# Gated delta rule on one Trainium2 core: the inverse of a 128-token chunk assembled ahead by two products for pairs of heads

## The chip, the cores and the metric

One core of a Trainium2 chip runs the whole layer in one launch. The metric is device time in microseconds (us), the median of three runs. TensorE is called PE below, VectorE DVE, ScalarE ACT, GpSimd POOL; SP is the queue from which this kernel issues all its DMAs.

## What is computed

The layer has a gated DeltaNet branch and a stick-breaking attention branch; both are projected, gated, merged and projected out. The change lies in the DeltaNet branch. For each of 4 heads a state of 128x128 is carried over chunks of the 2048 tokens; within a chunk a unit lower triangular system is solved:

```python
m = where(strict, beta[..., :, None] * kk * decay, 0.0)
sol = triangular_solve(eye + m, rhs, left_side=True, lower=True, unit_diagonal=True)
...
def step(state, inp):
    v_new = u_c - einsum('bhck,bhkv->bhcv', w_c, state)
    o = einsum('bhck,bhkv->bhcv', qd_c, state) + einsum('bhij,bhjv->bhiv', qk_c, v_new)
    state = state * ge_c[..., None, None] + einsum('bhck,bhcv->bhkv', kd_c, v_new)
    return state, o
```

The kernel works with chunks of 128 tokens, 16 in all (the reference's are 64; the result is the same).

## The kernel before

**Stages.** Projections of all columns of the input come first (tiles `pj`; weights and activations are split in two parts, so three matmuls stand for one product). While the last attention projections run, `dn_solve` (L671 to L711) inverts on DVE the two 64x64 diagonal blocks of all 16 x 4 triangular systems at once, one (chunk, head) in each partition, and stores them transposed in the scratch tensor `d_tt`. Then come attention, the recurrence over chunks (`dn_states`, L713) mixed with the last gate projections (`pj`) and with the up-projections (`up`, L913, tiles `y`), the rest of the up-projections, and the output projection (tiles `o`).

**One chunk** is `dn_chunk` (L780). `mm4` (L772) makes one product for each of the 4 heads, in plain f32, into one PSUM bank; a tile called `dn` is such a bank. A chunk has seven of them:

- two with `kq` and the state: the right-hand side `rn` (DVE, L788) and the first part of the output `o` (L791); POOL then scales the state (L792);
- three to apply the inverse: `tt` (the two 64x64 inverses on the diagonal) times `rn`, copied to `v1` by ACT (L796); `mo` (the coupling block, its only nonzero quarter) times `v1`, added to `rn` by DVE (L799); and `tt` times `rn` again, scaled into `w2` and `w` (L803, L804);
- one with `kt` that updates the state (L807), and one with `qk` that completes `o` (L809). POOL, ACT and DVE then normalise `o` (L811 to L819); four PE transposes and a store follow later (`tail`, L821).

**Loads.** `dn_load` (L752) brings a chunk's `kq`, `vn`, `tt` (two DMAs), `kt`, `qk` and `za`; `kq`, `vn`, `qk` and `za` have one buffer each. `mo` is loaded in `dn_chunk`.

**Order.** Each `yield` of `dn_chunk` ends a step; `dn_states` lets at least `LD` = 1.1 us of PE work of other kinds be recorded between two steps. PE work is chained in the order of recording, so PE's order is fixed: steps of the recurrence with groups of 6 `pj` matmuls or 12 `y` matmuls between them. Each other engine and SP run their instructions in one order too. `up` of 256 tokens may begin once the outputs of its two chunks are stored.

Of the kernel before, what the change touches and what calls it, by code (L numbers as in the profile page):

```python
# [8 lines left out]
F32 = mybir.dt.float32  # L9
# [4 lines left out]
ALU = mybir.AluOpType  # L14
# [4 lines left out]
P = 128  # L19
# [6 lines left out]
NH = 4  # L26
NC = S // P
# [3 lines left out]
HB = 64  # L31
# [6 lines left out]
class Block:  # L38


    def __init__(self, ctx, tc, ins, out):
        self.ctx, self.tc, self.nc = ctx, tc, tc.nc
        self.i = ins
        self.out = out
        dr = ctx.enter_context(tc.tile_pool(name="dr", bufs=1, space=DRAM))

        def scratch(name, n, shape):
            return [dr.tile(shape, F32, name=f"{name}{i}") for i in range(n)]

        self.d_kq = dr.tile([NC, P, NH, 2, P], F32, name="d_kq")  # L50
        self.d_kt = dr.tile([NC, P, NH, P], F32, name="d_kt")
        self.d_vn = dr.tile([NC, P, NH, P], F32, name="d_vn")
        self.d_qk = dr.tile([NC, P, NH, P], F32, name="d_qk")
        self.d_mt = dr.tile([NC, NH, P, P], F32, name="d_mt")
        self.d_tt = dr.tile([NC, NH, 2, HB, HB], F32, name="d_tt")
        self.d_za = scratch("d_za", NC, [P, NH * P])
        self.d_q = dr.tile([2, SH * SD, S], F32, name="d_q")
        self.d_k = dr.tile([2, SH * SD, S], F32, name="d_k")
        self.d_v = dr.tile([SH, P, NT, P], F32, name="d_v")
        self.d_zb = scratch("d_zb", 4, [P, S])  # L60
        self.d_g = scratch("d_g", S // OG, [P, KB, 2, OG])
        self.d_oa = dr.tile([4, P, S], F32, name="d_oa")
        self.d_ob = dr.tile([4, P, S], F32, name="d_ob")
        self.d_m = dr.tile([S // OG, P, KB, OG], F32, name="d_m")
        self.now, self.pending, self.back, self.credit, self.rate = 0, [], None, 0.0, 0.0
        self.op, self.lead, self.slot = None, 0, 0
        self.chain, self.last, self.clock, self.attended, self.zb_done = False, None, 0.0, False, 0
        self.consts()
# [602 lines left out]
    def dn_solve(self):  # L671
# [31 lines left out]
            nc.gpsimd.affine_select(bt, bt, pattern=[[-1, H], [1, n]], compare_op=ALU.not_equal, fill=1.0, base=0, channel_multiplier=0)  # L703
        zero = wk.tile([P, H, H], F32, name="zero", bufs=1)
        nc.vector.memset(zero, 0.0)
        for b in range(2):
            ls = slice(L * b, L * b + L)
            nc.sync.dma_start(t[:, b, 0:H], b1[ls])
            nc.sync.dma_start(t[:, b, H:HB, H:HB], b2[ls])
            nc.sync.dma_start(t[:, b, H:HB, 0:H], zero[ls])  # L710
        yield 1.0  # L711

    def dn_states(self):  # L713
# [1 line left out]
        st = wk.tile([P, NH, P], F32, name="state", bufs=1)  # L715
        nc.vector.memset(st, 0.0)
        tts = [wk.tile([P, NH, P], F32, name=f"tt{k}", bufs=1) for k in range(2)]
        mo = wk.tile([P, NH, P], F32, name="mo", bufs=1)
        for t in tts + [mo]:
            nc.gpsimd.memset(t, 0.0)  # L720
        tails, self.stored = [], 0

# [8 lines left out]
                self.stored += 1  # L731
                yield 0.0

        loads = self.dn_load(0, tts[0])
        yield from self.wait(self.clock + 9.0)
        for c in range(NC):
            yield from store(1)
            cur = loads
            steps = self.dn_chunk(c, cur, st, mo)
            for n, _ in enumerate(steps):  # L740
                if n == 1 and c + 1 < NC:
                    loads = self.dn_load(c + 1, tts[(c + 1) % 2])
                yield from store(2)
                yield 0.0
                yield from self.wait(self.clock + self.LD)
            tails.append((self.clock + 11, self.dn_tail))
        yield from store()

    def dt(self, name, n):
        return self.dk.tile([P, NH, P], F32, tag=name, name=name, bufs=n)  # L750

    def dn_load(self, c, tt):  # L752
        nc = self.nc
        kq = self.dk.tile([P, NH, 2, P], F32, tag="kq", name="kq", bufs=1)
        kt, vn, qk, za = self.dt("kt", 2), self.dt("vn", 1), self.dt("qk", 1), self.dt("za", 1)
        nc.sync.dma_start(kq, self.d_kq[c])
        nc.sync.dma_start(vn, self.d_vn[c])
        for b in range(2):
            bs = slice(HB * b, HB * b + HB)
            nc.sync.dma_start(tt[bs, :, bs], self.d_tt[c, :, b].rearrange("h x i -> x h i"))  # L760
        nc.sync.dma_start(kt, self.d_kt[c])
        nc.sync.dma_start(qk, self.d_qk[c])
        nc.sync.dma_start(za, self.d_za[c].rearrange("p (h d) -> p h d", h=NH))
        return kq, kt, vn, qk, za, tt

    def bank(self):
        return self.pt.tile([P, NH, P], F32, tag="tp", name="dn")
# [9 lines left out]

    LD = 1.1

    def dn_chunk(self, c, loads, st, mo):  # L780

        nc = self.nc
        kq, kt, vn, qk, za, tt = loads
        nc.sync.dma_start(mo[0:HB, :, HB:P], self.d_mt[c, :, 0:HB, HB:P].rearrange("h j i -> j h i"))
        ps = self.mm4(lambda h: kq[:, h, 0], lambda h: st[:, h])
        rn = self.dt("rn", 1)
        for h in range(NH):
# [2 lines left out]
        o = self.dt("o", 2)  # L790
        nc.vector.tensor_tensor(o, ps, self.bc(self.egc, c), ALU.mult)  # L791
        nc.gpsimd.tensor_tensor(st, st, self.bc(self.ge, c), ALU.mult)  # L792
        yield
        ps = self.mm4(lambda h: tt[:, h], lambda h: rn[:, h])
        v1 = self.dt("v1", 1)
        nc.scalar.copy(v1, ps)  # L796
        yield
        ps = self.mm4(lambda h: mo[:, h], lambda h: v1[:, h])
        nc.vector.tensor_tensor(rn, ps, rn, ALU.add)  # L799
        yield  # L800
        ps = self.mm4(lambda h: tt[:, h], lambda h: rn[:, h])
        w, w2 = self.dt("w", 1), self.dt("w2", 1)
# [430 lines left out]
```

## Time and profile before

| | |
|---|---|
| median of 3 runs | 2068.93 us (2068.79 to 2069.32) |
| profiled execution | 2067.06 us, its span 2065.3 us |
| PE busy | 2017.7 us, 98% of the span |
| DVE, POOL, ACT busy | 1399.9, 1023.6, 933.2 us |
| granted TensorE clock, mean | 0.997 of full |
| DMA | 286.71 MB, 139 GB/s over the span |
| recurrence, first to last `dn` instruction | 1535.8 to about 1784 us |

The span runs from the first to the last instruction; 1.8 us lie around it. A busy PE is not a PE at its peak: matmuls overlap, and what a group costs is read from where the next one starts. A row of the trace names the line, the engine, the operation and out<-in; an idle time in brackets or behind a bar is that just before the instruction, with what ended it.

### The profile page before, as it was taken

What the parts mean: (1) busy time and instruction counts of PE and PEld (TensorE: products, weight loads), DVE (VectorE), ACT (ScalarE), POOL (GpSimd) and SP (SyncE); (2) the same over time, 40 slices, a digit from 0 to 9 for tenths busy, and PEclk for the clock granted to TensorE, in tenths of its full rate; (3) what the DMA queues carried; (4) which work ended last, traced back from release to release, by engine and by line L of the source; (5) the groups of instructions that cost most, each with busy time, mean ns of one, the idle gap of its engine ahead of it and who ended that gap; (6) DMA issues with size and microseconds to landing.
All of it is one profiled execution on the core that took longest, in us unless ns stands there. A gap on an engine that the chain in (4) does not pass through costs nothing. (4 is left out here: it accounts for less than half of the span.)

```text
span 2065.3 us, 36611 instructions
## 1 busy us (share of the span) xinstructions
PE 2017.7 (98%) x12831; PEld 1810.2 (88%) x12831; DVE 1399.9 (68%) x2559; ACT 933.2 (45%) x1933; POOL 1023.6 (50%) x1200
## 2 busy tenths in 40 slices
PE   7999999999999999999999999999999999999999
PEld 7987887789999988888888888888888889999887
DVE  7356777777999318888888877877744466443753
ACT  6335655322222117767667766766733321211321
POOL 4336776533443205555555555555537654533564
PEclk9999999999999999999999999999999999999999
DMA  7213333226333553344664443443347787655552
GB/s 244 66 57 106 114 108 97 80 79 128 104 122 113 149 139 106 112 123 114 162 180 133 135 116 104 115 114 104 101 132 225 220 263 230 205 189 163 204 193 102
DMA packets 273511, 286.71 MB, mean 139 GB/s; under 512 B 48752, under 2 KB 206640, under 8 KB 272176
## 3 DMA queue, kind: packets, MB, share of 16 engines
q1 hardware_dynamic: 273328, 284.38, 46.4%
q8 instruction: 102, 1.67, 0.3%
q14 instruction: 81, 0.66, 0.1%
HBM read 181.54 MB, written 102.76 MB: 138 GB/s over the span
## 5 line engine op out<-in xcount | busy, mean ns | idle before, releaser
L1184 POOL TENSOR_TENSOR s<-s,r 128x512 f32<-128x512 f32 (+2 forms) x320 | 306.5, 958 | 321.5 <-DVE r L1180 315.1
L124 PE MATMUL pj<-xh,whi 128*128 128x512 f32 x1024 | 422.5, 413 | 1.9 <-DVE one L1053 1.9
L124 PE MATMUL pj<-xh,wlo 128*128 128x512 f32 x1024 | 405.4, 396 | 0.0
L124 PE MATMUL pj<-xl,whi 128*128 128x512 f32 x1024 | 404.8, 395 | 0.0
L124 PE MATMUL pj<-whi,xh 128*128 128x256 f32 (+1 forms) x1024 | 293.2, 286 | 1.0 <-ACT xh L380 1.0
L1180 DVE TENSOR_TENSOR_SCAN r<-z,carry,zero 128x512 f32<-128x512 f32 x192 | 245.8, 1280 | 69.2 <-ACT z L1178 57.7
L124 PE MATMUL pj<-wlo,xh 128*128 128x256 f32 (+1 forms) x1024 | 289.6, 283 | 0.2 <-DVE wlo L330 0.2
L124 PE MATMUL pj<-whi,xl 128*128 128x256 f32 (+1 forms) x1024 | 289.7, 283 | 0.0
L1177 ACT ACTIVATE s<-z 128x512 f32<-128x512 f32 (+2 forms) x320 | 171.5, 536 | 140.0 <-PE z L124 62.2
L124 PEld LDWEIGHTS pj<-xh,wlo 128*128 128x128 f32 x1024 | 192.9, 188 | 44.1
L124 PEld LDWEIGHTS pj<-xh,whi 128*128 128x128 f32 x1024 | 193.5, 189 | 28.9 <-issue 2.1
L124 PEld LDWEIGHTS pj<-xl,whi 128*128 128x128 f32 x1024 | 194.0, 189 | 27.4
L124 PEld LDWEIGHTS pj<-whi,xh 128*128 128x128 f32 x1024 | 194.2, 190 | 1.4 <-ACT xh L380 1.4
L124 PEld LDWEIGHTS pj<-wlo,xh 128*128 128x128 f32 x1024 | 194.4, 190 | 0.5 <-DVE wlo L330 0.5
L124 PEld LDWEIGHTS pj<-whi,xl 128*128 128x128 f32 x1024 | 194.0, 190 | 0.3 <-DVE xl L381 0.3
L1200 DVE TENSOR_TENSOR lo<-at,hi 128x512 fp32r<-128x512 f32 (+1 forms) x288 | 183.8, 649 | 14.1 <-ACT hi L1199 13.3
L124 PE MATMUL z<-kt,qt 128*128 128x512 f32 (+3 forms) x640 | 187.2, 374 | 0.9 <-DVE r L1180 0.6
L1199 ACT CAST hi<-at 128x512 fp32r<-128x512 f32 (+1 forms) x288 | 159.3, 566 | 60.3 <-PE at L128 55.2
L330 POOL TENSOR_TENSOR wlo<-wraw,whi 128x512 fp32r<-128x512 f32 (+2 forms) x66 | 115.8, 1755 | 123.6 <-ACT whi L329 102.7
L1178 ACT ACTIVATE z<-z 128x512 f32<-128x512 f32 (+2 forms) x320 | 170.4, 532 | 0.0
L128 PE MATMUL at<-ident,s 128*128 128x128 f32 x1088 | 165.2, 274 | 1.2 <-DVE lo L1200 0.5
L124 PE MATMUL y<-xh,xh 128*128 128x256 f32 x512 | 149.6, 292 | 3.2 <-DVE yt L929 3.2
(219 smaller groups left out, 4329.1 us busy)
## 6 DMA issues: line engine op xcount, KB each, us to landing
kt<-d_k SPq DMA_DIRECT2D x160, 128.0 KB, 2.9
vt<-d_v SPq DMA_DIRECT2D x80, 256.0 KB, 3.6
xt<-in_x_dram SPq DMA_DIRECT2D x32, 512.0 KB, 4.3
qt<-d_q SPq DMA_DIRECT2D x64, 256.0 KB, 5.4
d_g<-sg SPq DMA_DIRECT2D x128, 128.0 KB, 2.3
gt<-d_g SPq DMA_DIRECT2D x64, 256.0 KB, 3.3
wraw<-in_w_in_dram SPq DMA_DIRECT2D x56, 256.0 KB, 3.3
wraw<-in_w_in_dram SPq DMA_DIRECT2D x18, 512.0 KB, 4.0
```

The costliest lines, as they stand in the source:

```text
L124: self.pin(self.nc.tensor.matmul(out, lhsT, rhs, **kw))
L128: self.pin(self.nc.tensor.transpose(*args))
L330: (eng or nc.gpsimd).tensor_tensor(lo[:, ks, :n], raw[:, :, :n], hi[:, ks, :n].bitcast(F32), ALU.subtract)
L1177: nc.scalar.activation(s[:, :w], z[:, :w], AF.Sigmoid, scale=SD ** -0.5)
L1178: nc.scalar.activation(z[:, :w], z[:, :w], AF.Sigmoid, scale=-(SD ** -0.5))
L1180: nc.vector.tensor_tensor_scan(r[:, 0:w][:, ::-1], z[:, 0:w][:, ::-1], self.zero.to_broadcast([P, w]), init, ALU.mult, ALU.add)
L1184: nc.gpsimd.tensor_mul(s[:, :w], s[:, :w], r[:, 1:w + 1])
L1199: nc.scalar.copy(hi[:, c:], flat[:, c:])
L1200: nc.vector.tensor_tensor(lo[:, c:], flat[:, c:], hi[:, c:].bitcast(F32), ALU.subtract)
```

## The change

For a chunk the inverse of a 2x2 block triangular matrix is [[T1, 0], [N21, T2]], N21 a product of T2, the coupling block and T1. The change makes that corner ahead. `dn_solve` also writes the first 64x64 inverse of each system untransposed to a new scratch tensor `d_tn`: 32 small copies on ACT and 16 DMAs, through three slots of the scratch tile `stmp`. The new `dn_inverse` loads, for a chunk, the coupling blocks of two heads onto the diagonal of a 128x128 tile (`n12`, heads by b::2), the two inverses (`ends`) and `tt`; in two steps it makes two products of 64 columns each time (one for two heads): `n12` with `ends`, copied by ACT onto the diagonal of `yb`, and `yb` with `ends`, copied by ACT into the empty corner of `tt`. `dn_chunk` then applies `tt` once: the products with `mo` and the second one with `tt`, the copy to `v1` and the addition L799 are gone. `qk` and `za` get a second buffer, the next chunk's loads are issued one step earlier, and `dn_inverse` of chunk c+1 runs inside chunk c.

```diff
@@ dn_solve
+        for q in range(16):
+            nat = tmp[0:L, q % 3 * 4 * HB:(q % 3 + 1) * 4 * HB].rearrange("p (i x) -> p i x", x=HB)
+            qs = slice(4 * q, 4 * q + 4)
+            nc.scalar.copy(nat[:, :, 0:H], b1[0:L, :, qs].rearrange("p x i -> p i x"))
+            if q < 8:
+                nc.scalar.copy(nat[:, :, H:HB], zero[0:L, 0:4])
+            else:
+                nc.scalar.copy(nat[:, :, H:HB], b2[0:L, :, 4 * q - H:4 * q - H + 4].rearrange("p x i -> p i x"))
+            nc.sync.dma_start(self.d_tn.rearrange("c h i x -> (c h) i x")[:, qs], nat)
+            yield 0.25
@@ dn_states
-        loads = self.dn_load(0, tts[0])
+        between = [self.dn_inverse(c, tts[c]) for c in range(2)]
+        loads = self.dn_load(0)
         yield from self.wait(self.clock + 9.0)
+        for _ in between.pop(0):
+            yield from self.wait(self.clock + self.LD)
         for c in range(NC):
             yield from store(1)
-            cur = loads
-            steps = self.dn_chunk(c, cur, st, mo)
+            steps = self.dn_chunk(c, loads, tts[c % 2], st)
             for n, _ in enumerate(steps):
-                if n == 1 and c + 1 < NC:
-                    loads = self.dn_load(c + 1, tts[(c + 1) % 2])
+                if n == 0 and c + 1 < NC:
+                    loads = self.dn_load(c + 1)
+                elif between:
+                    next(between[0], None)
+                if n == 1 and c + 2 < NC:
+                    between.append(self.dn_inverse(c + 2, tts[c % 2]))
                 yield from store(2)
                 yield 0.0
                 yield from self.wait(self.clock + self.LD)
+            between[:1] = []
@@ dn_load
-        kt, vn, qk, za = self.dt("kt", 2), self.dt("vn", 1), self.dt("qk", 1), self.dt("za", 1)
+        kt, vn, qk, za = self.dt("kt", 2), self.dt("vn", 1), self.dt("qk", 2), self.dt("za", 2)
-        for b in range(2):
-            bs = slice(HB * b, HB * b + HB)
-            nc.sync.dma_start(tt[bs, :, bs], self.d_tt[c, :, b].rearrange("h x i -> x h i"))
+    def dn_inverse(self, c, tt):
+        nc = self.nc
+        n12 = self.n12[c % 2]
+        ends = self.dk.tile([P, 2, 2, HB], F32, tag="ends", name="ends", bufs=2)
+        for b in range(2):
+            bs = slice(HB * b, HB * b + HB)
+            nc.sync.dma_start(n12[bs, :, bs], self.d_mt[c, b::2, 0:HB, HB:P].rearrange("h j i -> j h i"))
+            nc.sync.dma_start(ends[bs, 0], self.d_tn[c, b::2].rearrange("h i x -> i h x"))
+            nc.sync.dma_start(ends[bs, 1], self.d_tt[c, b::2, 1].rearrange("h x i -> x h i"))
+            nc.sync.dma_start(tt[bs, :, bs], self.d_tt[c, :, b].rearrange("h x i -> x h i"))
+        def pairs(lhsT, e):
+            ps = self.bank()
+            for u in range(2):
+                self.mm(ps[:, u, 0:HB], lhsT[:, u], ends[:, e, u], start=True, stop=True)
+            return ps
+        def steps():
+            ps = pairs(n12, 0)
+            for b in range(2):
+                bs = slice(HB * b, HB * b + HB)
+                nc.scalar.copy(self.yb[bs, :, bs], ps[bs, 0:2, 0:HB])
+            yield
+            ps = pairs(self.yb, 1)
+            for b in range(2):
+                nc.scalar.copy(tt[0:HB, b::2, HB:P], ps[HB * b:HB * b + HB, 0:2, 0:HB])
+            yield
+        return steps()
@@ dn_chunk
-        nc.sync.dma_start(mo[0:HB, :, HB:P], self.d_mt[c, :, 0:HB, HB:P].rearrange("h j i -> j h i"))
...
-        yield
-        ps = self.mm4(lambda h: tt[:, h], lambda h: rn[:, h])
-        v1 = self.dt("v1", 1)
-        nc.scalar.copy(v1, ps)
-        yield
-        ps = self.mm4(lambda h: mo[:, h], lambda h: v1[:, h])
-        nc.vector.tensor_tensor(rn, ps, rn, ALU.add)
         yield
         ps = self.mm4(lambda h: tt[:, h], lambda h: rn[:, h])
```

The order of instructions is the same on PE up to the recurrence. PE before, one chunk of the stretch with gate projections; the tiles are named above, and each "..." stands for the rest of a group of 6 `pj` matmuls:

```order
L124 MATMUL dn<-state,kq 128x128 x8
L124 MATMUL pj<-xh_138,whi 128x512
...
L124 MATMUL dn<-rn,tt_18575 128x128 x4
...
L124 MATMUL dn<-v_18789,mo 128x128 x4
...
L124 MATMUL dn<-rn,tt_18575 128x128 x4
...
L124 MATMUL dn<-w_18842,kt 128x128 x4
L124 MATMUL dn<-w,qk 128x128 x4
L128 MATMUL dn<-ident,o 128x128 x4
```

PE after, one chunk of the same stretch:

```order
L125 MATMUL dn<-state,kq 128x128 x8
L125 MATMUL pj<-xh_136,whi 128x512
...
L125 MATMUL dn<-rn,tt_18624 128x128 x4
L125 MATMUL dn<-ends,n_18625 128x64 x2
...
L125 MATMUL dn<-w_19125,kt 128x128 x4
L125 MATMUL dn<-w,qk 128x128 x4
L125 MATMUL dn<-ends,yb 128x64 x2
...
L129 MATMUL dn<-ident,o 128x128 x4
```

Two groups of four products are gone and two short groups are there, joined to others; a chunk now holds 18 or 27 `pj` (later 36 or 54 `y`) where it held 30 (60). In the whole recurrence 225 `pj` and 360 `y` stand where there were 237 and 591; the other 231 `y` follow it.

SP before, from one chunk's load of `kq` on (`raw` are weights of the up-projection, `d_g` stores of gates):

```order
L756 DMA kq<-d_kq 128x1024
L757 DMA vn<-d_vn 128x512
L668 DMA d_g_86<-sg 128x256
L668 DMA d_g_87<-sg 128x256
L784 DMA mo<-d_mt 64x4x64
L763 DMA za<-d_za_65 128x512
L760 DMA tt_18574<-d_tt 64x4x64
L889 DMA raw<-in_w_up_a_dram 128x512
...
L761 DMA kt<-d_kt 128x512
...
L762 DMA qk<-d_qk 128x512
```

SP after, from one chunk's load of `kq` on:

```order
L777 DMA kq<-d_kq 128x1024
L778 DMA vn<-d_vn 128x512
L931 DMA raw<-in_w_up_a_dram 128x512
L781 DMA za<-d_za_67 128x512
L795 DMA tt_18623<-d_tt 64x4x64 x2
L792 DMA n_18626<-d_mt 64x2x64
...
L779 DMA kt<-d_kt 128x512
L780 DMA qk<-d_qk 128x512
L793 DMA ends<-d_tn 64x2x64
L794 DMA ends<-d_tt 64x2x64
```

A chunk had 9 DMAs of its own, 3 of them over 64 partitions; it has 14, 8 of them over 64 partitions (`n`, `ends`, `tt`, two or four of each), with the loads and stores of other work between them as before. At the start of the recurrence 16 DMAs of `dn_inverse`, for two chunks, stand ahead of the first `kq`, which before came first.

## Rows read from the trace of the kernel before

**Rows 1.** The page's head and its busy times by engine.

```profile
span 2065.3 us, 36611 instructions
PE 2017.7 (98%) x12831; PEld 1810.2 (88%) x12831; DVE 1399.9 (68%) x2559; ACT 933.2 (45%) x1933; POOL 1023.6 (50%) x1200
```

**Rows 2.** Timeline of PE: start us, us, engine, line, out<-in, form, count [idle <-releaser].

```profile
1645.86 1.05 PE L124 MATMUL dn<-w,kt 128*128 128x128 f32 x8
1646.74 1.06 PE L124 MATMUL dn<-w,qk 128*128 128x128 f32 x8
1647.64 0.60 PE L128 MATMUL dn<-ident,o 128*128 128x128 f32 x4
1647.99 0.48 PE L124 MATMUL pj<-xh,whi 128*128 128x512 f32 x1
1648.31 0.40 PE L124 MATMUL pj<-xl,whi 128*128 128x512 f32 x1
1648.54 0.40 PE L124 MATMUL pj<-xh,wlo 128*128 128x512 f32 x1
1648.78 0.28 PE L124 MATMUL y<-xh,xh 128*128 128x256 f32 x1
1648.90 0.28 PE L124 MATMUL y<-xl,xh 128*128 128x256 f32 x1
```

**Rows 3.** Groups by line of 1535 to 1784 us, PE: busy, mean ns | idle before, releasers.

```profile
L124 PE MATMUL dn<-rn,tt 128*128 128x128 f32 x256 | 35.0, 280 | 5.4 <-DVE rn L799 3.0 <-DVE rn L788 2.4
...
L124 PE MATMUL dn<-v,mo 128*128 128x128 f32 x128 | 17.3, 278 | 4.3 <-ACT v L796 4.3
```

**Rows 4.** Tile tp, products of 64 columns: ns min/median/max, first and last start us.

```profile
L124 PE MATMUL tp<-g,tri_le x2: 218/246/275, 138.6 to 138.6; 128*128 128x64 f32 x2
...
L124 PE MATMUL tp<-g,ones x2: 275/275/275, 139.0 to 139.1; 128*128 128x64 f32 x2
```

**Rows 5.** DMA of 1535 to 1784 us: packets, MB, share of 16 engines; median us to landing.

```profile
q1 hardware_dynamic: 52100, 56.34, 73.5%
...
kq<-d_kq SPq DMA_DIRECT2D x15, 512.0 KB, 4.7
```

**Rows 6.** DMA of 360 to 420 us, where few packets are under 512 B.

```profile
q1 hardware_dynamic: 8448, 4.98, 27.7%
```

**Rows 7.** DMA of 420 to 480 us, where half of them are.

```profile
DMA packets 13264, 5.38 MB, mean 90 GB/s; under 512 B 7117, under 2 KB 13261, under 8 KB 13261
...
q1 hardware_dynamic: 13261, 5.34, 43.6%
```

**Rows 8.** DMA of 1700 to 1715 us, the busiest 15 us of the recurrence.

```profile
q1 hardware_dynamic: 4177, 4.11, 90.1%
```

**Rows 9.** Tiles kq and tt on SP: ns of an issue, min/median/max, first and last.

```profile
L756 SPq DMA_DIRECT2D kq<-d_kq x16: 319/320/457, 1530.9 to 1743.4; - x16
L760 SPq DMA_DIRECT2D tt<-d_tt x32: 580/586/1430, 1531.9 to 1736.9; - x32
```

**Rows 10.** Timeline of SP at the start of the recurrence.

```profile
1530.86 0.46 SPq L756 DMA_DIRECT2D kq<-d_kq  x1
1531.37 0.42 SPq L757 DMA_DIRECT2D vn<-d_vn  x1
```

**Rows 11.** Timeline of PE where the recurrence begins.

```profile
1535.83 1.39 PE L124 MATMUL dn<-state,kq 128*128 128x128 f32 x11
```

**Rows 12.** Timeline of PE at the first matmuls after the attention projections.

```profile
744.44 0.77 PE L124 MATMUL pj<-xh,whi 128*128 128x512 f32 x1 [1.92 <-DVE one L1053]
745.00 0.63 PE L124 MATMUL pj<-xl,whi 128*128 128x512 f32 x1
```

**Rows 13.** Two windows: us, PE, PEld, DVE, ACT, POOL busy; PEclk, DMA share, GB/s.

```profile
745.00:760.00 15.00, 15.00 (x62) 12.31 (x61) 1.38 (x2) 1.20 (x2) 0.00 (x0) 0.91 0.86 213
...
1650.00:1700.00 50.00, 45.55 (x378) 45.14 (x378) 31.97 (x61) 12.62 (x26) 26.14 (x27) 0.97 0.83 257
```

**Rows 14.** Timeline of POOL: the weights of the next projection made ready.

```profile
708.91 1.30 POOL L330 TENSOR_TENSOR wlo<-wraw,whi 128x512 fp32r<-128x512 f32 x1 [3.65 <-ACT whi L329]
```

More of the change, by code (lines that the diff above doesn't have):

```diff
@@ L55, in __init__ @@
         self.d_tt = dr.tile([NC, NH, 2, HB, HB], F32, name="d_tt")
+        self.d_tn = dr.tile([NC, NH, HB, HB], F32, name="d_tn")
         self.d_za = scratch("d_za", NC, [P, NH * P])
@@ L717, in dn_states @@
         tts = [wk.tile([P, NH, P], F32, name=f"tt{k}", bufs=1) for k in range(2)]
-        mo = wk.tile([P, NH, P], F32, name="mo", bufs=1)
-        for t in tts + [mo]:
+        self.n12 = [wk.tile([P, 2, P], F32, name=f"n12{k}", bufs=1) for k in range(2)]
+        self.yb = wk.tile([P, 2, P], F32, name="yb", bufs=1)
+        for t in tts + self.n12 + [self.yb]:
             nc.gpsimd.memset(t, 0.0)
@@ L750, in dt, with dn_load @@
         return self.dk.tile([P, NH, P], F32, tag=name, name=name, bufs=n)
-    def dn_load(self, c, tt):
+    def dn_load(self, c):
         nc = self.nc
         kq = self.dk.tile([P, NH, 2, P], F32, tag="kq", name="kq", bufs=1)
-        kt, vn, qk, za = self.dt("kt", 2), self.dt("vn", 1), self.dt("qk", 1), self.dt("za", 1)
+        kt, vn, qk, za = self.dt("kt", 2), self.dt("vn", 1), self.dt("qk", 2), self.dt("za", 2)
         nc.sync.dma_start(kq, self.d_kq[c])
         nc.sync.dma_start(vn, self.d_vn[c])
-        for b in range(2):
-            bs = slice(HB * b, HB * b + HB)
-            nc.sync.dma_start(tt[bs, :, bs], self.d_tt[c, :, b].rearrange("h x i -> x h i"))
         nc.sync.dma_start(kt, self.d_kt[c])
@@ L763, in dn_load @@
         nc.sync.dma_start(za, self.d_za[c].rearrange("p (h d) -> p h d", h=NH))
-        return kq, kt, vn, qk, za, tt
+        return kq, kt, vn, qk, za
+    def dn_inverse(self, c, tt):
[24 more added lines that the diff above has]
+        return steps()
     def bank(self):
@@ L778, with dn_chunk @@
     LD = 1.1
-    def dn_chunk(self, c, loads, st, mo):
+    def dn_chunk(self, c, loads, tt, st):
         nc = self.nc
-        kq, kt, vn, qk, za, tt = loads
-        nc.sync.dma_start(mo[0:HB, :, HB:P], self.d_mt[c, :, 0:HB, HB:P].rearrange("h j i -> j h i"))
+        kq, kt, vn, qk, za = loads
         ps = self.mm4(lambda h: kq[:, h, 0], lambda h: st[:, h])
```

## Prediction

> **What bounds the kernel now.** I read the page's head first: PE is busy for 98% of the span [rows 1], so time is won by taking work from PE or by removing one of its few waits, and nearly every wait of another engine costs nothing. The chain of waits, looked at next, runs through PE there too. Then the timeline of PE within the recurrence, where the change lies: what a group costs is the distance to the start of the next. Four products of `mm4`, eight instructions, take 0.89 us (1645.86 to 1646.74, 1646.74 to 1647.64), the four transposes 0.35, a `pj` matmul 0.23, a `y` matmul 0.12 [rows 2]. The groups by line of 1535 to 1784 us give PE's waits: 5.4 us ahead of `tt` (3.0 of it for L799) and 4.3 ahead of `mo`, all for the copy to `v1` [rows 3].
>
> **Products removed.** Two `mm4` in each of 16 chunks, 16 x 2 x 0.89 [rows 2] = 28.5 us. They lie in PE's one order, with other work before and behind, so all of it is on the path: -28.5.
>
> **Products added.** Four f32 products of 64 columns for each chunk, eight instructions. In the order they stand directly behind other f32 products. The one place with 64 columns before is tile `tp`: six instructions start between 138.6 and 139.1 us [rows 4], some 0.1 us each, as long as the 0.11 of 128 columns [rows 2]. So half the columns save nothing: 16 x 8 x 0.111 = +14.2. The lower bound, halved with the columns, is +7.1. The Trainium skill (TensorE: Matmul & The Clock Gate, Back-to-back issue gap) has an isolated matmul of 64 columns take about 60 cycles, or 25 ns. By that the 128 instructions would come to an estimated 3 us and the sum to 11 us less; the rows speak against it.
>
> **Waits removed.** The copy to `v1` and L799 leave the path, and with them 4.3 + 3.0 us [rows 3]: -7.3. What can be late next are the ACT copies to `yb` and `tt`: behind their product PE has other work for 3.2 us (6 `pj` and two `mm4`: 1.4 + 1.8) and 4.6 us (two groups of 6 `pj` and two `mm4`), where `v1` had the 1.4 us of 6 `pj`. ACT runs in order and stands behind casts that wait for loads, so some may come back; bounds 0 and 7.3, taken as 0, since the cover is more than twice as long.
>
> **The start of the recurrence.** Sixteen DMAs over 64 partitions now stand ahead of the first `kq`. SP needs 0.586 us for the issue of such a one [rows 9] and some 0.07 between two: 16 x 0.66 = 10.5 us. The first `kq` was issued at 1530.9 [rows 10] and is then issued at 1541.4; with 4.7 us to landing [rows 5] it is there at 1546.1. PE came to its first product at 1535.8 [rows 11], and now has two short groups (0.9) and 12 `pj` (2.8) ahead of `kq`: 1539.5, so it waits up to 6.6 us. If the smaller ones (12 of the 16 have half of `tt`'s rows) cost 0.40, it is 4.4. I take 5. A wait also costs clock: after the idle 1.92 us at 744 the next matmul started 0.56 us after the first, not 0.23 [rows 12], and the granted clock of that 15 us was 0.91 [rows 13], part of it at the lower of the two levels (1.2 and 2.4 GHz), so about 1.3 us were lost. I add 1: together +6, bounds +2 and +8.
>
> **A shorter chunk.** By the order a chunk holds 5 `mm4`, the two short groups (0.44 each), the transposes and 22.5 `pj` or 45 `y` on average: 4.45 + 0.89 + 0.35 + 5.2 = 10.9 us, where it was 7 x 0.89 + 0.35 + 30 x 0.23 = 13.5 without waits. Everything that feeds a chunk must come faster.
>
> SP: 14 DMAs of its own, 8 of them at 0.586 and 6 at 0.32 to 0.46 [rows 9, 10], and 4 to 6 of other work. From one `kq` to the next this is 8.5 to 12.8 us, 10.7 on average over 14 chunks, where it was 8.4. That is 98% of the chunk, so SP has no time left for waits. Followed by hand, chunk by chunk, each `kq` goes out 0 to 1.5 us after its one buffer is free, and with 4.7 us to landing it is there 1.6 to 5 us before PE needs it. So SP alone holds nothing up, with little to spare.
>
> DMA engines: in 249 us each was busy for 73.5% [rows 5], 183 us. The `y` that move behind the recurrence take about 5.0 MB of loads and stores with them, at 183 / 56.3 = 3.25 us a MB, 16 us. Added are 512 packets of 256 B a chunk (`ends`). Between 360 and 420 us 8448 packets took 27.7% of 16 engines [rows 6], 31 ns each; from 420 to 480 us, with 7117 under 512 B among 13261 packets, 43.6% [rows 7], also 32 ns. So 16 x 512 x 32 ns / 16 = 16 us, and the need stays at 183 us. PE would go through the recurrence in 194 us: 225 x 0.231 + 360 x 0.119 + 16 x (5.34 + 0.35) and the 2.8 us of 12 `pj` make 189, times 1.027, as the same sum for before falls short of what was measured. Engines busy for 94% were seen nowhere with this mixture; the busiest 15 us had 90.1% [rows 8]. At 90% it is 203 us: loads are late by +9 in all. Lower bound 0 (the walk along SP), upper bound 22: the recurrence's 53.9 MB at the 257 GB/s of its fullest 50 us [rows 13] take 210 us, and the small packets 6 more.
>
> **Cover that must hold.** In `dn_solve` 32 copies and 16 stores precede the next projection's weights in SP's order; between the first store of `d_tt` and the first of these loads stand 8 stores of `d_v` where 4 stood, paced by PE at two in 5.7 us. The loads move by some 11.5 us. The first half of the weights was ready at 710.2 [rows 14] and is used at 744.4 [rows 12], so 22 us remain: 0. Without that cover PE would wait up to 11 us. POOL has 5.4 us of 10.9 for a chunk, and up to 3.5 more while weights of the up-projections come: 0. The second part of the up-projections is the same work, later: 0.
>
> **Sum.** -28.5 + 14.2 - 7.3 + 6 + 9 = -6.6. The profiled execution took 2067.06 us (span 2065.3 and 1.8 around it), so 2060.5 in its frame; the median of the runs is 1.9 higher: **2062.3 us**.
>
> **Rivals.** *The loads are in time* (0 for the +9, +2 at the start): -19.6, 2049.3 us. For it speaks the walk along SP, against it the 94%. Chance 0.12; a further 0.02 for short products at half the price, as their columns would have it: 7.1 us less than the forecast, 2055.2. By the skill's figure above that one would be 2051.
>
> *The waits take it all.* The change does what it says on PE, and the 15.6 us that are left after the start go to late `kq`, to ACT's copies behind casts, and to POOL's queue: 1.0 us a chunk. For it speaks that SP, DMA and PE would all be over 90% busy, each in a fixed order, and that PE was idle for 4.45 of 50 us before where the loads were densest [rows 13]. Within 4 us of before, 2069. Chance 0.24.
>
> *The DMA engines set the pace, slower than before.* `kq` has one buffer: it is asked for when its last product ends, and the next one starts 8 us later in a short chunk. If it lands after more than 8 us rather than 4.7, PE stands still by the difference in each chunk. With small packets at 64 ns rather than 32 the engines need 199 us, at 90% 221 us, 27 in place of 9: +11.4, 2080.3. It is slower once the lateness exceeds 1.0 us a chunk, and by over 0.2% from 1.2. For it speaks the busy share, against it the two stretches with equal 31 and 32 ns. Chance 0.24. The Trainium skill (DMA: Bandwidth & Descriptors, Specifications) says that below 512 B a transfer is a read-modify-write; by that 64 ns would be an estimate for 256 B. Against it, rows 6 and 7 show no dearer packet, though a 256 B one moves fewer bytes in that time.
>
> That the change does not do what it says can be left out: the order shows the groups gone and the new ones covered.
>
> **The numbers.** 0.2%, or 4.1 us, is about what a measurement of this kernel can tell from no change. The forecast (-4 to -15) has 0.38; with 0.14 for the faster rivals, faster has 0.52, within 0.2% 0.24, slower 0.24. The range goes from 2050 (loads in time) to 2080 (the slow rival); each side leaves out about 0.1.
>
> **What would show it.** Right: per chunk 10.9 us of PE's work in the timeline, short groups at 0.44 us, the first `kq` product some 6 us late, DMA share near 0.9 in the recurrence, PE's idle time there near 18 us with DMA as its releaser through `kq` or `vn`. Wrong: short groups at 0.2 us; PE waiting for ACT `yb` or `tt`; a chunk of more than 12 us; a wait at the projection that begins at 744 us.

## The result and the profile after

The change is slower: 2083.9 us (median of 4 runs, 2080.6 to 2086.7) against 2069.1 for the kernel before in the same sitting; ratio 1.0074, 95% interval 1.0060 to 1.0089. The profiled execution took 2085.2 us; the page's head and its first busy times answer to [rows 1]:

```profile
span 2083.5 us, 36549 instructions
PE 2016.1 (97%) x12703; PEld 1804.7 (87%) x12703; DVE 1385.2 (66%) x2543; ACT 950.6 (46%) x2013; POOL 1021.8 (49%) x1202
```

PE has 128 instructions less, and yet nearly the same busy time: a matmul counts as busy for longer when the clock is lower (below, a `pj` counts 0.63 us behind a wait, 0.40 in [rows 2]). The windows of the recurrence say where the time went. First the one of the kernel before beside [rows 13], then three of the change (us, busy time of PE, PEld, DVE, ACT, POOL; PEclk, DMA share, GB/s):

```profile
1600.00:1650.00 50.00, 46.65 (x309) 41.55 (x308) 24.79 (x51) 16.80 (x32) 30.17 (x27) 1.00 0.71 219
```

```profile
1535.00:1600.00 65.00, 57.78 (x360) 50.97 (x358) 20.39 (x45) 14.42 (x35) 25.81 (x27) 0.97 0.72 213
1600.00:1650.00 50.00, 41.38 (x248) 37.09 (x247) 21.69 (x46) 18.12 (x40) 36.76 (x33) 0.86 0.84 256
1650.00:1700.00 50.00, 44.01 (x307) 40.40 (x307) 25.37 (x54) 17.77 (x41) 28.79 (x26) 0.97 0.75 227
```

Added over six such windows from 1535 to 1850 us, PE is idle for 32.1 us where it was 14.4. The clock loses about 14.0 us (each window times what its PEclk lacks to 1) where it lost 3.0. With the 14.3 us of PE work that the order removes this makes -14.3 + 17.7 + 11.0 = +14.4 us; the medians differ by 14.8. So the saving is there, and twice as much is given back in waits and clock.

The groups of 1535 to 1784 us on PE, which answer to [rows 3]:

```profile
L125 PE MATMUL dn<-state,kq 128*128 128x128 f32 x256 | 33.9, 290 | 6.2 <-DMA kq<-d_kq 6.2
L125 PE MATMUL dn<-rn,tt 128*128 128x128 f32 x128 | 18.7, 291 | 9.0 <-ACT xh L941 3.8 <-ACT oT L868 3.8 <-issue 1.3
L125 PE MATMUL dn<-w,kt 128*128 128x128 f32 x128 | 17.9, 284 | 6.1 <-DVE w L845 6.1
L129 PE MATMUL dn<-ident,o 128*128 128x128 f32 x64 | 10.2, 283 | 6.3 <-POOL o L861 6.3
L125 PE MATMUL dn<-ends,n 128*128 128x64 f32 x64 | 9.7, 278 | 0.4 <-DMA ends<-d_tn 0.4
L125 PE MATMUL dn<-ends,yb 128*128 128x64 f32 x64 | 9.3, 270 | 0.0
```

The waits ahead of `mo` and for L799 are gone, and the short products hardly wait (0.4 and 0.0 us). The 6.2 us at `kq` are mostly the start of the recurrence (4.92). New waits stand at `tt`, `kt` and the transposes, and their releasers are ACT, DVE and POOL. One of them, followed back (timeline of all engines, rows left out between):

```profile
1598.53 0.62 ACT L932 CAST xh<-raw 128x512 fp32r<-128x512 f32 x1 [7.32 <-DMA raw<-in_w_up_a_dram]
1599.23 2.52 POOL L933 TENSOR_TENSOR xl<-raw,xh 128x512 fp32r<-128x512 f32 x2 [5.09 <-ACT xh L932]
...
1601.69 1.05 POOL L853 TENSOR_TENSOR o<-o,rq 128x512 f32<-128x512 f32 x1
...
1602.78 0.63 ACT L855 ACTIVATE v<-o 128x512 f32<-128x512 f32 x1 [0.82 <-POOL o L853]
1603.44 0.69 DVE L857 TENSOR_REDUCE ss<-v 128x4 f32<-128x512 f32 x1 [8.91 <-ACT v L855]
1604.05 1.12 DVE L837 SCALAR_TENSOR_TENSOR rn<-dn,egc,vn 128x128 f32<-128x128 f32 x4
```

A weight `raw` of the up-projections comes late, so ACT stands at its cast; POOL stands behind ACT and scales `o` late; ACT squares it late, DVE reduces it late, and `rn`, which has nothing to do with that weight, is behind it in DVE's order. PE then waits (timeline of PE):

```profile
1604.49 2.04 PE L125 MATMUL dn<-rn,tt 128*128 128x128 f32 x8 [3.17 <-ACT oT L868]
...
1608.04 0.63 PE L125 MATMUL pj<-xh,wlo 128*128 128x512 f32 x1
1608.47 0.63 PE L125 MATMUL pj<-xh,whi 128*128 128x512 f32 x1
```

The releaser named is a copy that ended at 1603.89, 0.6 us before; it is L837, the last of the chain above. Behind the idle 3.17 us a `pj` matmul starts 0.43 us after the one before, not 0.23 as in [rows 2]: the clock has gone to the lower of its two levels.

Three more waits lead back to a cast on ACT in the same way (timeline of all engines): 1.33 us at 1686.72 to one that stood 3.97 us for `raw`, and 2.51 us at 1664.19 and 3.27 us at 1715.38 to casts that stood 4.51 and 5.41 us for `ot`, the outputs of the two branches that the up-projection reads. The four make 10.3 of the 32.1 us. Ahead of the longest wait, 5.46 us at the transposes at 1641.49, POOL had three L933 of 1.3 us each in its order from 1632.87 on. The other waits were not followed.

Why `raw` is late shows on SP (timeline of SP):

```profile
1587.84 0.58 SPq L793 DMA_DIRECT2D ends<-d_tn  x1
1588.47 0.60 SPq L794 DMA_DIRECT2D ends<-d_tt  x1
1589.12 0.60 SPq L792 DMA_DIRECT2D n<-d_mt  x1
1589.76 0.60 SPq L793 DMA_DIRECT2D ends<-d_tn  x1
1590.41 0.61 SPq L794 DMA_DIRECT2D ends<-d_tt  x1
1591.12 0.54 SPq L869 DMA_DIRECT2D d_oa<-oT  x1
1591.76 0.45 SPq L777 DMA_DIRECT2D kq<-d_kq  x1
1592.30 0.40 SPq L778 DMA_DIRECT2D vn<-d_vn  x1
1592.79 0.86 SPq L931 DMA_DIRECT2D raw<-in_w_up_a_dram  x2
```

Five inverse DMAs in a row hold SP for 3.3 us, with no pause between, and `raw` is behind them.

### The profile page after: what moved, and what is told of

Its sections match the earlier page's. It is cut to its first block, busy times and chain, and to the rows that moved or that the text cites. A ratio compares the mean times of both kernels' runs of the same rounds, so it can differ in the third digit from the quotient of the medians.

```text
span 2083.5 us, 36549 instructions
## 1 busy us (share of the span) xinstructions
PE 2016.1 (97%) x12703; PEld 1804.7 (87%) x12703; DVE 1385.2 (66%) x2543; ACT 950.6 (46%) x2013; POOL 1021.8 (49%) x1202
## 5 line engine op out<-in xcount | busy, mean ns | idle before, releaser
L1242 DVE TENSOR_TENSOR lo<-at,hi 128x512 fp32r<-128x512 f32 (+1 forms) x288 | 183.9, 649 | 15.7 <-ACT hi L1241 14.8
```

The lines of the kernel that those rows point to most:

```text
L1242: nc.vector.tensor_tensor(lo[:, c:], flat[:, c:], hi[:, c:].bitcast(F32), ALU.subtract)
```

## The experiments

The diffs are shortened: `...` stands for what is left out, and the comments are added. My theory after this was that SP's issue time is the cause; the rivals were the added bytes and packets on the DMA engines, the short chunk itself, and the start of the recurrence. The DMAs of a chunk are the recurrence's own, its store among them. Idle is PE's idle time from 1535 to 1850 us, lost clock the sum formed above; both are from the one profiled execution of each kernel, which can lie at either end of its runs (for e15 it was the fastest, for e16 and e17 the slowest). The runs come from six sittings, in which the kernel before took 2066.8 to 2069.1 us; each ratio is to the kernel before in its own sitting. Where two kernels of different sittings are compared, their medians can be some 2 us off, and the ratios decide.

| kernel | DMAs a chunk, SP + ACT | median us | ratio to before, 95% | idle | lost clock |
|---|---|---|---|---|---|
| before | 9 | 2069.1 | | 14.4 | 3.0 |
| change | 14 | 2083.9 | 1.0060 to 1.0089 | 32.1 | 14.0 |
| e4 no inverse loads | 6 | 2057.0 | 0.9943 to 0.9969 | 16.1 | 3.3 |
| e6 bytes in one DMA | 7 | 2057.3 | 0.9931 to 0.9966 | 16.6 | 6.3 |
| e5 eight empty issues | 14 | 2068.5 | 0.9989 to 1.0011 | 23.6 | 8.2 |
| e17 bytes in one, seven empty | 14 | 2077.1 | 1.0027 to 1.0056 | 31.9 | 13.2 |
| e13 bytes in eight, none read | 14 | 2079.2 | 1.0041 to 1.0075 | 26.5 | 12.9 |
| e7 before, no loads of `tt`, `mo` | 6 | 2068.0 | 0.9995 to 1.0018 | 14.5 | 1.5 |
| e12 before, five empty issues | 14 | 2078.6 | 1.0044 to 1.0087 | 21.2 | 6.5 |
| e2 first loads ahead | 14 | 2085.3 | 1.0070 to 1.0109 | 32.7 | 13.5 |
| e9 inverse loads later | 14 | 2084.0 | 1.0057 to 1.0104 | 32.5 | 16.8 |
| e1 longer gaps | 14 | 2076.6 | 1.0038 to 1.0075 | 26.5 | 10.5 |
| e3 inverse loads by ACT | 6 + 8 | 2072.1 | 1.0016 to 1.0037 | 25.1 | 8.2 |
| e10 six by ACT | 6 + 6 | 2069.5 | 0.9999 to 1.0023 | 21.7 | 10.2 |
| e11 and stores by ACT | 5 + 7 | 2071.2 | 1.0000 to 1.0030 | 24.0 | 4.8 |
| e8 packed | 11 | 2069.3 | 1.0000 to 1.0021 | 19.4 | 4.5 |
| e14 packed, stores shared | 11 | 2061.4 | 0.9959 to 0.9979 | 17.6 | 5.0 |
| e15 and `n12` by ACT | 9 + 2 | 2057.3 | 0.9941 to 0.9971 | 14.6 | 1.5 |
| e16 and longer gaps | 9 + 2 | 2050.7 | 0.9899 to 0.9938 | 14.9 | 3.0 |
| e18 and still longer | 9 + 2 | 2047.6 | 0.9884 to 0.9917 | 9.6 | 3.0 |

### The transfers, taken away on either side (e4, e7)

```diff
+        if c < 2:
+            self.ends = getattr(self, "ends", []) + [self.dk.tile(...)]
+        ends = self.ends[c % 2]
-        for b in range(2):
+        for b in range(2 if c < 2 else 0):     # e4; in e7 the same line for tt in dn_load
-        nc.sync.dma_start(mo[0:HB, :, HB:P], ...)     # e7
+        if c == 0:
+            nc.sync.dma_start(mo[0:HB, :, HB:P], ...)
```

> Leaves out the eight inverse DMAs of chunks 2 to 15 (the short products run on the operands of chunks 0 and 1), so 112 issues on SyncE and 1280 packets of 256 B a chunk are gone, fewer than even the kernel before has (3 small DMAs a chunk); everything else stands. If the added transfers (issue or bytes) are the cause of the late loads, TensorE's idle time falls to below 15 us and the time to 2055 +- 4, below the kernel before. If the short chunk alone squeezes the in-order queues of ScalarE, GpSimd and VectorE, most of the idle time stays and the time is 2072 or above.

> The kernel before, with the loads of tt and mo left out for chunks 2 to 15 (1 to 15 for mo): three issues and 768 packets of 256 B a chunk less. If the kernel before had room for its loads (13.5 us a chunk against 9 issues), the time stays within 2 us of 2067, and the change's own gain on TensorE, read against the change without loads, is 10 us or more. If the loads of the recurrence weigh on the kernel before too, it falls to 2055 to 2062, and the products' own gain is less than that.

Without them the change takes 2057.0 us: the inverse loads cost 27 us by the medians and 24 by the ratios, most of the 29 that were to be explained (-14.3 forecast for the products, +14.8 measured). The kernel before gains nothing by the loss of its own (2068.0), so it had room for them. The difference of the two, 11 us, is what the products are worth when loads are no matter, the start of the recurrence included. For a view of it, the `raw` weights and their casts from 1560 to 1660 us, of the change and then of e4:

```profile
L931 SPq DMA_DIRECT2D raw<-in_w_up_a_dram x8: 367/408/554, 1578.5 to 1602.9; - x8
  DMA raw<-in_w_up_a_dram: 14.0, 5
  DMA raw<-in_w_up_b_dram: 11.3, 7
DMA to landing us min/median/max: 2.9/4.0/6.3
```

```profile
L933 SPq DMA_DIRECT2D raw<-in_w_up_a_dram x5: 332/382/439, 1581.7 to 1590.6; - x5
  DMA raw<-in_w_up_a_dram: 6.0, 5
  DMA raw<-in_w_up_b_dram: 5.0, 3
DMA to landing us min/median/max: 3.0/4.4/6.1
```

ACT's idle time for these two weights falls from 25.3 to 11.0 us, though a transfer takes no less time from issue to landing (median 4.4 against 4.0). They were late because they were issued late: the first of the eight of `in_w_up_a` went out at 1578.5 us in the change, at 1553.2 in e4 (three of them before this window). The sum of such idle time does not rank the kernels: with the weights of the output projection, and from 1535 to 1784 us, it is 37.9 us in the change, 37.0 in e4 and 20.0 before. What counts is whether something that PE needs stands behind the cast.

### Issues or bytes (e5, e6, then e13, e17)

```diff
+            for b in range(8):     # e5: 64 partitions x 4 bytes, tile dum
+                nc.sync.dma_start(self.dum[...64 partitions, 1 column], self.i["w_in"][...])
+            nc.sync.dma_start(self.dum, ...)     # e6: [128, 8, 64], 1024 pieces of 256 B
```

> The kernel without the inverse loads (2057 us), with eight DMAs a chunk put back in their place on SyncE, each 64 partitions by one number of 4 bytes: the issues are there again, the bytes are not (the inverse loads are left out for chunks 2 to 15, as before). The 27 us between that kernel and the change are then divided: if SyncE's issue time makes them, the time goes to 2072 or above; if bytes and packets make them, it stays at 2061 or below. In between both have a part.

> The kernel without the inverse loads (2057 us), with one DMA a chunk in their place that carries 1024 pieces of 256 bytes from the projection weights (four fifths of the pieces of the eight inverse DMAs): the bytes are there again, seven of the eight issues are not (the inverse loads are left out for chunks 2 to 15). If bytes and packets make the 27 us, four fifths of it come back and the time goes to 2074 or above; if SyncE's issue time makes them, it stays at 2061 or below.

The bytes alone cost 0.3 us, the empty issues 11.5 (9 by the ratios). Bytes are out as a cause by themselves, and 11.5 is not the whole of 27. One reservation on e6: nothing in the kernel holds its fourteen DMAs to the chunks, and they went out between 1552.1 and 1620.6 us, one in about 5 us, so its later chunks had none. While they ran the DMA share was 0.85 and 0.88 (the first two windows), and PE was idle for 7.0 us in them, in e4 for 5.9. The issues on SP, ns min/median/max, of e5 and of e6 between 1560 and 1660 us:

```profile
L796 SPq DMA_DIRECT2D dum<-in_w_in_dram x71: 465/514/1894, 1560.8 to 1659.4; - x71
```

```profile
L795 SPq DMA_DIRECT2D dum<-in_w_in_dram x12: 378/384/458, 1564.5 to 1620.6; - x12
```

Two more runs for the rest. e13 has the eight DMAs with their 256 B pieces into a tile that nobody reads; e17 has 896 pieces in one DMA and seven empty issues:

```diff
+                nc.sync.dma_start(d[:, 0:2], self.d_mt[c, b::2, 0:HB, HB:P]...)     # e13, for b in 0, 1
+                nc.sync.dma_start(d[:, 2:4], self.d_tn[c, b::2]...)
+                nc.sync.dma_start(d[:, 4:6], self.d_tt[c, b::2, 1]...)
+                nc.sync.dma_start(d[:, 6:8], self.d_tt[c, b::2, 0]...)
+            nc.sync.dma_start(self.dum, ...)     # e17: [128, 7, 64]
+            for b in range(7):
+                nc.sync.dma_start(self.dot[...64 partitions, 1 column], self.i["w_in"][...])
```

> The kernel without the inverse loads (left out for chunks 2 to 15), with eight DMAs a chunk in their place on SyncE that fetch what the change fetches (the two of tt cut to two heads: 1024 pieces of 256 B), into a tile that nothing reads. Issues and bytes are there, the waits for tt, n12 and ends and the products' dependence are not. If an issue with 256-byte pieces costs SyncE more than one with nothing, the time goes from 2068.5 (issues alone) to 2077 or above; if the other 15 us are the waits and the dependence, it stays at 2066 to 2071.

> The kernel without the inverse loads (left out for chunks 2 to 15), with eight issues a chunk on SyncE again, but the bytes apart from them: one DMA with 896 pieces of 256 B and seven of 64 partitions by 4 bytes. If the small DMAs that carry pieces are dear by themselves, the time is near that of the empty issues, 2066 to 2071. If a full order on SyncE and full DMA engines add to each other whoever carries the bytes, it is 2075 or above.

Both come to 2077 to 2079, and their DMAs are spread to 1712 us and beyond. So pieces need not lie in the small DMAs, and neither the waits for free buffers nor the products' dependence makes most of the rest: with fourteen issues a chunk, some 1000 pieces of 256 B cost another 9 to 11 us (8.5 to 12 by the ratios), and with seven (e6) none. Why the two add, the runs don't show: e17 (PE idle 31.9 us) lands its `kq` after 4.9 us in the median from 1600 to 1700, e6 after 5.2. The last 5 us to the change (2083.9) would go to what e13 left out: two heads of `tt`, the waits and the dependence. They are not told apart, and by the ratios, whose intervals overlap, they are 3 us and not clear of the noise.

### The kernel before with as many issues (e12)

```diff
+            for b in range(5):     # in dn_load, ahead of tt
+                nc.sync.dma_start(self.dum[...64 partitions, 1 column], self.i["w_in"][...])
```

> The kernel before with five DMAs a chunk of 64 partitions by 4 bytes added on SyncE (14 issues a chunk, as the change has, at the old pace of 13.5 us a chunk). If the issues hurt only where the chunk is shortened, the time stays within 2 us of 2067. If SyncE is near its limit in the kernel before too (it waits for 88 of 200 us there, and the five take some 45 of them), it rises to 2070 to 2078.

It is slower by 11 us, and the row that [rows 3] had at 4.3 us now reads (PE, 1535 to 1784 us):

```profile
L124 PE MATMUL dn<-v,mo 128*128 128x128 f32 x128 | 19.4, 299 | 12.4 <-ACT v L801 12.4
```

The number of issues hurts at the old pace too. ACT, which makes `v1` in one order with the casts, waits 30.5 us for `raw` in this stretch (12.7, 9.1 and 8.7 for the three weights) where it waited 20.0; that these waits are what makes `v1` late is read from the orders, not tested apart. The SP order of the kernel before has room for its nine DMAs a chunk, not for fourteen.

### The other readings (e2, e9, e1)

```diff
-        between = [self.dn_inverse(c, tts[c]) for c in range(2)]
         loads = self.dn_load(0)
+        between = [self.dn_inverse(c, tts[c]) for c in range(2)]     # e2
-                if n == 1 and c + 2 < NC:
+                if n == 2 and c + 2 < NC:     # e9
-    LD = 1.1
+    LD = 1.5     # e1
```

> Only the order of the first loads is changed: chunk 0's kq, vn, kt, qk and za are issued ahead of the 16 small DMAs of the first two inverses. If the start costs what I put down for it (a wait of 4.9 us for kq at 1549.8, and the lower clock behind it), the time falls by 4 to 7 us to about 2078. If kq was late because the stretch is full of transfers anyway, or the wait only moves to the first short products, it stays within 2 us of 2084.

The start falls as a cause. The wait for `kq` is gone and stands elsewhere (PE, 1535 to 1850 us):

```profile
L125 PE MATMUL dn<-state,kq 128*128 128x128 f32 x256 | 31.3, 275 | 0.2 <-DMA kq<-d_kq 0.2
...
L125 PE MATMUL dn<-ends,n 128*128 128x64 f32 x64 | 10.4, 292 | 7.2 <-DMA ends<-d_tn 4.2 <-ACT oT L868 3.0
```

> The change with the eight inverse DMAs of chunk c+2 written one step later in chunk c (behind kt and qk, in place of behind the product that reads tt), still on SyncE: the same issues and bytes. If part of the 27 us is SyncE standing at these DMAs until TensorE has freed tt, n12 and ends, with kq, raw and ot queued behind (some 10 us of such waits are in the change's trace), the time falls by 5 us or more, to 2079 or below. If issue time alone counts, it stays at 2081 to 2087.

No change: where in the chunk SP stands at these DMAs is not the cause either.

> Work on TensorE unchanged; each of the three gaps of a chunk gets 9 projection matmuls where the change has 6 (LD 1.5 in place of 1.1), so that a chunk takes about 13 us of TensorE again, as before the change (13.5). If the shortened chunk is the cause (the orders of ScalarE, GpSimd, VectorE and SyncE have 10.9 us a chunk where they had 13.5), the idle time of TensorE between 1535 and 1850 us falls from 32 to about 14 us, the lower clock's loss from 14 to about 4, and the time to 2060 +- 4. If the loss comes from the added transfers or from the start whatever the pace, it stays at 2080 to 2086.

This is neither of the two readings. Longer gaps give back 7 us by the medians, but 3.5 by the ratios, with intervals that overlap those of the change; idle time stays at 26.5 us. If pace has a part here it is a small one, and the loads stay late.

### Issued by ACT (e3, e10, e11)

```diff
-            nc.sync.dma_start(n12[bs, :, bs], ...)     # e3: all eight lines, and n == 2 as in e9
+            nc.scalar.dma_start(n12[bs, :, bs], ...)
-            nc.sync.dma_start(ends[bs, 0], ...d_tn...)     # e10: ends[:, u] = [T1 | T2] in 512 B
-            nc.sync.dma_start(ends[bs, 1], ...d_tt...)
+            nc.scalar.dma_start(ends[bs], self.d_en[c, b::2].rearrange("h x e i -> x h (e i)"))
-            nc.sync.dma_start(self.d_oa..., oT)     # e11, as e10; the stores of sg likewise
+            nc.scalar.dma_start(self.d_oa..., oT)
```

> The same eight inverse DMAs per chunk, with the same bytes and packets, are issued by ScalarE in place of SyncE (one step later in the chunk, so that the product that reads tt lies behind TensorE already). If SyncE's issue time is the cause (14 DMAs, 8 of them at 0.58 us, 98% of a chunk), the loads of raw and ot are no longer late, TensorE's idle time between 1535 and 1850 falls from 32 us to below 18 and the time to 2062 to 2070. If bytes and packets are the cause (transfers land later), or the short chunk squeezes the other engines' orders, it stays at 2080 or above; ScalarE's own issue time (about 4.6 us a chunk) can add to that.

> Both right-hand sides of a head's short products lie beside each other in DRAM (512 B in one piece), so that two DMAs of 64 partitions take the place of four, and the six that are left are issued by ScalarE, one step later. SyncE has 6 issues a chunk of the recurrence's own, fewer than in the kernel before (9). If SyncE is the cause, the time goes to 2055 to 2062, below the kernel before; ScalarE's issue time (six by 0.6 us, 3.6 us a chunk) is the price, and if that weighs, it is 2064 to 2072.

> The kernel of the run before, and in the recurrence the stores of sg and oT, which ScalarE itself has just written, are issued by ScalarE too: SyncE has neither their issue nor their wait (it waits 8 us for sg and 6 us for oT where it has time). If SyncE's order is still the limit, the time falls by another 2 to 5 us; if ScalarE's own time has become the limit, it rises.

The same bytes through another queue take 12 us off the change (10 by the ratios), which lies between the two readings, and idle time stays at 25.1 us where I expected less than 18. Two DMAs less give 2.6 us more, within the noise; the stores moved to ACT give nothing. My 2055 to 2062 for e10 was wrong, and the price named beside it (2064 to 2072) was paid: ACT is in the chain that feeds PE, and its issues delay it, as I read the rows; no run tests that apart. Two groups of e11 (PE, 1535 to 1850 us) that had 6.3 and 0.0 in the change:

```profile
L129 PE MATMUL dn<-ident,o 128*128 128x128 f32 x64 | 9.8, 276 | 7.3 <-POOL o L861 7.3
L125 PE MATMUL dn<-ends,yb 128*128 128x64 f32 x64 | 9.5, 274 | 5.4 <-ACT yb L807 5.4
```

### Fewer issues (e8, e14, e15, e16, e18)

```diff
-            nc.sync.dma_start(ends[bs, 0], self.d_tn[c, b::2]...)
-            nc.sync.dma_start(ends[bs, 1], self.d_tt[c, b::2, 1]...)
+        nc.sync.dma_start(ends, self.d_en[c])     # e8: 128 partitions x 1 KB, heads 2b, 2b+1
-                    nc.sync.dma_start(d..., b1[ls])
+                    (nc.sync, nc.scalar)[u].dma_start(d..., b1[ls])     # e14: dn_solve's stores
-            nc.sync.dma_start(n12[bs, :, bs], ...)
+            nc.scalar.dma_start(n12[bs, :, bs], ...)     # e15, and n == 2
+    LD = 1.5     # e16; e18: 1.95
```

> The change with heads paired 2b and 2b+1, and both right-hand sides of the short products stored as one array of 1 KB per partition, so that one DMA of 128 packets takes the place of four with 512 packets of 256 B: 11 DMAs a chunk in place of 14, 896 packets in place of 1280, the same bytes. By either theory of the transfers (issue time, or packets) it takes a part of the 27 us away: 3 of 8 issues would be some 10 us, 384 of 1280 packets some 8 us, so 2070 to 2076, and near the kernel before. If only the bytes count, it stays at 2080 or above.

> The kernel with 11 DMAs a chunk in place of 14 (2069.3 us), where half of the stores of the solving stage are issued by ScalarE: that kernel reached the recurrence 5 us later than the change, since SyncE had 28 stores more there, and took only 212 us from the first product to the last transposes (the change 233). If the 5 us come back, 2063 to 2066, below the kernel before; if not, 2069.

> As the run before, with the two DMAs of n12 issued by ScalarE, one step later in the chunk: SyncE has 9 issues a chunk, as in the kernel before, ScalarE 2. If SyncE is the limit, another 2 to 5 us go, to 2058 to 2063; if ScalarE's issue time costs as much as it saves (as six on ScalarE did), it stays at 2063 to 2068.

> As the run before, with 9 projection matmuls in a gap in place of 6 (LD 1.5). If the short gaps leave VectorE, ScalarE and GpSimd too little time even where the loads are there, it is 2 to 5 us faster than the run before; if the loads were the whole cause, it is the same within 2 us.

> As the kernel with one packed DMA, n12 on ScalarE and 9 projection matmuls in a gap (2050.7 us), with 12 in a gap (LD 1.95): the recurrence takes about 15 us a chunk and ends later than in the kernel before. If the chain has all the time it needs with 9, this is the same or slower, as less work is left to cover the last chunks: 2050 to 2056. If the products' waits still stand behind the short gaps, it is 2046 to 2049.

Each step goes the way that SP's theory says. Three issues less a chunk give 14.6 us (13 by the ratios), although with 28 more stores in `dn_solve` PE reaches its first recurrence product only at 1545.9 us (change 1541.0). e8 also has 384 pieces of 256 B less a chunk, so it does not tell issues from pieces; it came out a little faster than either reading had. With half of those stores issued by ACT it gets there at 1536.6, and e14 is below the kernel before. With nine issues on SP, as before the change, the clock loses 1.5 us in the profiled run; the ten runs of e15 spread from 2052.8 to 2064.5, and this was the fastest. Then the gaps count: 9 `pj` in place of 6 give 6.6 us. With 12 it is another 3.1, in another sitting and with intervals that overlap, so that step is not clear of the noise. The groups of e18 (PE, 1535 to 1784 us) beside those of the change:

```profile
L125 PE MATMUL dn<-state,kq 128*128 128x128 f32 x256 | 32.3, 281 | 0.0
L125 PE MATMUL dn<-w,kt 128*128 128x128 f32 x128 | 17.1, 276 | 2.6 <-DVE w L853 2.6
L125 PE MATMUL dn<-rn,tt 128*128 128x128 f32 x128 | 17.1, 275 | 0.0
L129 PE MATMUL dn<-ident,o 128*128 128x128 f32 x64 | 10.0, 281 | 0.0
```

Its DMA share over the six windows is 0.78, the change's 0.74 and the kernel before's 0.73: a mean share of 0.74 was no limit by itself. e18 is the version that beats both: 2047.6 us, 1.0% below the kernel before, with the change's products. The kernel before was not run with wider gaps, so how much of the 1.0% is the gaps' alone is not shown.

## Why the prediction was wrong

I said 2062.3 us, within 2050 to 2080, and gave slower 0.24. Step by step:

- **Products removed and added** (-28.5 + 14.2): right. Four short instructions take 0.37 us in the recurrence, a little under the 0.44 of the sum (timeline of PE):

```profile
1593.64 0.56 PE L125 MATMUL dn<-ends,yb 128*128 128x64 f32 x4
1594.01 0.48 PE L125 MATMUL pj<-xh,whi 128*128 128x512 f32 x1
```

That is 0.09 us an instruction, and the row of before was the better guide. The Trainium skill (TensorE: Matmul & The Clock Gate, Back-to-back issue gap) gives about 25 ns for an isolated matmul of 64 columns; the trace does not agree with that for these f32 products. The medians less idle time and lost clock agree: 2051.7 before, 2037.8 for the change, 14 less.

- **Waits removed** (-7.3): too large by about half even without the loads. The two waits went, but others stand ahead of `kt`, `tt` and `yb` behind gaps of 6 `pj`: without inverse loads idle time is 16.1 us against 14.4, and 5.0 of it is the start's wait for `kq`, so 3.3 are gained. With 12 `pj` in a gap (e18) it is 4.8 us.
- **The start** (+6): the wait was as long as forecast, 4.92 us at `kq` and 0.38 at the first short group, in part by luck: PE came to it at 1544.9 us and not at 1539.5, and `kq` let it go on at 1549.8 and not at 1546.1. It can't be had back by order alone (e2).
- **A shorter chunk, SP**: this is the step that failed. "So SP alone holds nothing up, with little to spare" came from a walk that followed `kq` alone. What else stands in SP's order was left out: `raw` and `ot` came late, and ACT, POOL and DVE, each in one order, carried that to `rn` and `w`. The prediction names this way ("ACT runs in order and stands behind casts that wait for loads, so some may come back") and takes it as 0, as it does POOL. The inverse loads cost 24 to 27 us, and e5 to e17 tie them to SP's order: the issues alone for 9 to 11.5, with the small pieces for 18 to 22. Nor was SP at 98%: from 1541 to 1775 us its issues add up to about 170 of 234 us (121 before), as a chunk took some 14.6 us in place of 10.9, and in the rest it stood waiting. e5 issues as long (172) and is 15 us faster, so the issue time is not the whole of it.
- **DMA engines** (+9): wrong cause. I expected a share near 0.9 and late `kq`; the share was 0.74, `kq` landed after 5.1 us in the median where it was 4.7, and 1024 pieces in one DMA cost 0.3 us (e6). That pieces cost 9 to 11 us beside fourteen issues (e13, e17) is near the +9 by luck, as the term came from the engines' busy share. The Trainium skill (DMA: Bandwidth & Descriptors, Specifications) says that a transfer below 512 B is a read-modify-write. With room on SP no run shows a price for it; whether it has a part in the 9 to 11 us is open.
- **The clock** (+1): wrong in size. It lost 11 us more than before. In 15 us from 1600, with the wait of 3.17, the granted clock was 0.77, which is 3.4 us, and as much in 15 us from 1636, with the wait of 5.46; in the 15 us that begin just before the waits of 2.51, 3.27 and 4.92 us it was 0.89, some 1.7 us each, and behind the two of 1.33 (from 1686) it was 1.00. I had counted one such wait; there were several.
- **Copies on ACT and POOL** (0 and 0): the copies held (`ends,yb` and `ends,n` wait 0.0 and 0.4), POOL did not (6.3 at the transposes, 5.46 of them at once).
- **Cover of the solving stage** (0): PE reached its first recurrence product at 1537.0 to 1541.0 us in the change and in those experiments that keep its stores and its first loads in place, at 1535.8 to 1536.5 in the three kernels built on before. With its stores shared by two queues it was 1536.6 (e14). So 1 to 5 us lay here that I had put at nothing.

Of the rivals, the one of late loads with "ACT's copies behind casts" and "POOL's queue" came nearest in mechanism. It added 1.0 us a chunk to what stands when nothing is late (2053.3); measured from there it was 1.9, (2083.9 - 2053.3) / 16.

## What to carry to other kernels

An issuing queue is an engine with an order: sum its issue times for the stretch, and where they and its waits fill the stretch, follow the transfer that is last in line, not the one that the change is about. Before splitting an operand into blocks, lay it out so that one DMA over all partitions fetches it; here that, two DMAs and half of the stores given to ACT, and longer gaps turned +0.74% into -1.0%. And where PE's waits lengthen, price the clock behind them too: here it was 11.0 us beside 17.7 us of waits.

## What the runs showed of the hardware

An issue's length does not follow the bytes. The same profile view has, in the median, `kq` (128 partitions, 512 KB) at 0.32 us before the change [rows 9] and 0.45 behind it, one DMA of 1024 pieces over 128 partitions at 0.38 (e6), an issue of 64 partitions by 4 bytes at 0.51 (e5), 64 partitions with 256 B pieces at 0.58 to 0.60 (e13), and 1 KB on each of 128 partitions (e14, 1560 to 1760 us) at 0.38:

```profile
L800 SPq DMA_DIRECT2D ends<-d_en x12: 319/382/396, 1562.7 to 1701.2; - x12
```

The Trainium skill (DMA: Bandwidth & Descriptors, Issuing engines are not separate DMA queues) says that issuing from several engines saves only the issue time, usually small beside the DMA. The trace agrees for one DMA: 0.6 us of issue beside some 3 us to landing. For the queue it was not small: eight such issues a chunk, moved to ACT (e3), were worth 10 to 12 us. And small pieces and many issues, cheap or moderate apart (0.3 and 11.5 us), cost 18 to 22 together; that stays without an explanation.
